# A decoder block on one core: the last output block's chain in column halves, its roots on ScalarE and VectorE, and two weight sums in the output stage

## The chip, the core and the metric

The kernel runs on one core of a Trainium2 chip. The metric is device time in microseconds: the median of three runs of the kernel before is 1132.89 us (1131.26 to 1133.38). One more execution was profiled. It took 1129.9 us, its span on the engines is 1128.1 us, and every time in the text that is read from an instruction is in us from that span's start. TensorE is called PE in the profile, VectorE DVE, ScalarE ACT, GpSimd POOL, and SyncE, which issues the DMAs, SP.

## What is computed

One transformer block over 1024 tokens of width 1024, in fp32. `rms_norm` divides by the root of the mean square and multiplies by a gain.

```python
h = rms_norm(x, g_attn_pre[l]) * (1 + sc_a) + sh_a
proj = h @ w_in[l]
...
mixed = jnp.concatenate([rms_norm(oa, g_mix_a[l]), rms_norm(ob, g_mix_b[l])], axis=-1)
y = mixed @ w_out[l]
x = x + gt_a * rms_norm(y, g_attn_post[l])

h = rms_norm(x, g_mlp_pre[l]) * (1 + sc_m) + sh_m
y = jnp.square(jax.nn.relu(h @ w_up[l])) @ w_down[l]
x = x + gt_m * rms_norm(y, g_mlp_post[l])
```

`oa` and `ob` are the results of two attention mixers with 512 columns each; the hidden width of the MLP is 4096.

## The kernel before

The kernel has three stages. Input projection and attention take the first 395 us. The output stage (`w_out`, both norms, the residual) follows to about 498 us. The MLP fills the rest.

**Products in parts.** A matrix product is made of three TensorE passes. Each operand is split into a high part, a cast by ScalarE, and a low part, the difference by VectorE, which needs the cast. The passes are high by high, high by low and low by high. In the MLP `split` (L1855 on) makes the parts: the cast is L1868 and the low part L1875, or L1866 and L1872 where an operand comes in two pieces of columns.

**The output stage.** `out_block` runs for eight blocks of 128 tokens, numbered 0 to 7. It loads the mixers' result (`o_sb`, L1625) and the residual (`x_sb`, L1629), makes the parts `oh` (ScalarE, L1638) and `ol` (VectorE, L1641), and squares and sums the mixers' result for their norms: a square on ScalarE (L1643), two additions on VectorE (L1647, L1648), a tiny product `pm_o` on TensorE (L1654), and a root, which is a first step on VectorE (`rs_t`, L1662) and a power of -0.5 on GpSimd (L1664). The product with `w_out` (`y_ps`, L1680 to L1682) is 16 groups of three matmuls; ScalarE (L1695) and VectorE (L1701) bring its halves of 512 columns to `y_sb`.

Then comes the block's chain. ScalarE squares `y` and sums (L1708); VectorE makes `rs_t` (L1717); GpSimd takes the power (L1719); VectorE multiplies by root and gate (L1723) and adds the residual (L1726), which SP stores (L1728); ScalarE squares again (L1708), `rs_t` and power follow again (L1717, L1719), and ScalarE scales by the root (`xn`, L1734). TensorE transposes `xn` (`px`, L1743, eight transposes), and ScalarE (L1759) and VectorE (L1762) scale, shift and store the result in quarters of the MLP's left operand: "11" and "12" are tokens 0 to 511 with either half of the features, "21" and "22" are tokens 512 to 1023. Each quarter lies in two tiles, 0 and 1.

**The MLP.** It multiplies in seven products per half of a pass instead of eight, in the order P1, P2, P6, P5, P7, P3, P4. P1 takes left quarter "11" with weight quarter "11", P2 takes "12" with "21"; both need only tokens 0 to 511. P6 takes S2 with T2. S1 = "21" + "22" and S2 = S1 - "11" are sums of left quarters, which need all tokens (`first_sums`, L1994, L1999, L2017); T1 = "12" - "11" and T2 = "22" - T1 are sums of weight quarters (`add_up`, L2037). In the first half T1 is written over weight quarter "11", whose parts must be made first, and the additions are queued when P6 is set up. The matmuls are L2104 to L2106, the results are read by L2138 to L2144.

**What sets the order.** A list scheduler in the kernel (`Sched`) fixes, when the program is built, the order of instructions of each engine. It knows a modelled duration of each step, its dependences, its tokens for memory, and a number `prio`; on each engine `pick` takes the step that can start earliest, with a handicap by `prio`. On the chip each engine runs its list in that order, so an instruction that waits holds up all behind it on its engine, and DMAs on SP's list too. On TensorE the last block's `px` stands behind 45 matmuls after block 6's `px` (all but one group of three of them from P1), and the other 45 matmuls of P2 behind it.

The first weight quarters are loaded in the order `RAW` (L2216), each behind the store of one block: the first behind block 2's, the last behind block 5's (L1849).

Of the kernel before, what the change touches and what calls it, by code (L numbers as in the profile page):

```python
# [10 lines left out]
F32 = mybir.dt.float32  # L11
# [171 lines left out]
class Step:  # L183
    __slots__ = ("dur", "emit", "deps", "takes", "gives", "prio", "seq", "ev", "alts", "after", "kind", "gone", "n", "lag")


class Sched:
# [11 lines left out]
    def step(self, dur, emit, deps=(), takes=(), gives=(), prio=5, after=None, kind="", n=1, lag=0.0):  # L199
        o = Step()  # L200
        o.n, o.lag = n, lag
        o.dur, o.emit, o.deps, o.takes, o.gives = dur, emit, deps, takes, gives
        o.prio, o.after, o.kind, o.ev, o.gone = prio, after, kind, Ev(), False
        o.seq = self.seq
        self.seq += 1
        return o
# [37 lines left out]
    def give_out(self, e, o, start):  # L244
# [12 lines left out]
        o.ev.t = end + o.lag  # L257
# [8 lines left out]
    def pick(self, e):  # L266
        best = None
        q = self.queue[e]
# [92 lines left out]
def hybrid_block(ctx: ExitStack, tc: tile.TileContext, x, positions, w_ada, b_ada, g_attn_post, w_in, w_out,  # L361
# [1226 lines left out]
    def open_h2():  # L1588
# [4 lines left out]
        ph2.right = pool("ring_r", 24, "right")  # L1593
        r_stg.give(sc.clk["PE"], NSTG2)
        r_raw.give(sc.clk["PE"], 10)
# [21 lines left out]

    def out_block(tb):
        b = {}

        late = tb >= TB - 2

# [88 lines left out]
        def norm(col, dep):  # L1711
            bx = []

            def f1():
# [6 lines left out]
        e = op("ACT", t_sb(D) + AP_COST, f_sq(0, True), ey, prio=1)  # L1721
        e = norm(0, e)
        e = op("DVE", t_dv(D), lambda: V.scalar_tensor_tensor(b["y"][:], b["y"][:], b["st"][:, 1:2], ph2.gate[:],  # L1723
                                                              ALU.mult, ALU.mult), [e, ph2.e_gate],
               gives=[(r_u, 1)] if tb == TB - 1 else [], prio=1)
        e = op("DVE", t_dv(D), lambda: V.tensor_tensor(b["y"][:], b["y"][:], b["xt"][:], ALU.add), [e, ex],  # L1726
               gives=[(r_stg, 1)], prio=1)
        e_x2[tb] = load(lambda: nc.sync.dma_start(x2_dram[tb][:], b["y"][:]), 524288, [e], prio=-2)  # L1728
        e = op("ACT", t_sb(D) + AP_COST, f_sq(2, False), [e], prio=1)
        e = norm(2, e)  # L1730

        def f_xn():
            b["xn"] = ring_l("xn2", F32)
            A.mul(b["xn"][:], b["y"][:], b["st"][:, 3:4])  # L1734
        exn = op("ACT", t_sb(D) + AP_COST, f_xn, [e], takes=[(ph2.r_xn, 1)], prio=1)
        ph2.pending_y = getattr(ph2, "pending_y", []) + [(exn, e_x2[tb], r_u if late else ph2.r_y)]
        et = []
        for kg in range(2):
# [5 lines left out]
            et.append(pe_op("xt", 0.43, f_t, [exn], takes=[(r_t, 1)],  # L1744
# [28 lines left out]
    def free_y():  # L1773
        for p_ in list(getattr(ph2, "pending_y", [])):
            if p_[0].t is not None and p_[1].t is not None:
                p_[2].give(max(p_[0].t, p_[1].t))
                ph2.pending_y.remove(p_)
# [56 lines left out]
    def load_raw(h, q):  # L1834
# [5 lines left out]
        for j in range(2):  # L1840
# [8 lines left out]
            deps = [halves[h - 1].e_b["T2"][j]] if h else [e_x2[2 + RAW.index(q)]]  # L1849
# [5 lines left out]
    def split(prio, rec, side, src, deps, free, pieces=None):  # L1855
# [3 lines left out]
        for i, c in enumerate(pieces or (slice(0, 512),)):  # L1859
            for j in range(2):  # L1860
# [21 lines left out]
                e1 = op("ACT", t_as(n), hi, d + (evs[j] or []), takes=[] if i else [(r_hl, 1)], prio=prio)  # L1882
                evs[j] = [e1, op("DVE", t_dv(n), lo, [e1], prio=prio,
# [24 lines left out]
    def sums(h, p):  # L1908
# [5 lines left out]
        if p == "P1":  # L1914
            fr.update({"T1": joins(r_raw, 2), "T3": joins(r_raw, 1), "B22": joins(r_raw, 3), "T4": joins(r_raw, 1),
                       "T2": joins(r_raw, 2)})
# [17 lines left out]
        if p == "P6":  # L1934
            sum_(t.b, t.e_b, eb, r_raw, None, "T1", "12", "11", ALU.subtract, [], t.sp["B", "11"], "11")
            sum_(t.b, t.e_b, eb, r_raw, ring_r, "T2", "22", "T1", ALU.subtract, [fr["B22"], fr["T1"]], None, None)
# [15 lines left out]
    def prep(h, p, rec):  # L1952
# [8 lines left out]
        fb = [fr["B22"]] if b == "22" else [fr[b]] if b in last_b else []  # L1961
# [65 lines left out]
    def add_up(prio, tiles, evs, ev, ring, new, out, x, y, alu, free, before, place):  # L2027
# [254 lines left out]
```

## Time and profile before

| what | us |
|---|---|
| median of the runs shown | 1132.89 (1131.26 to 1133.38) |
| the profiled execution | 1129.9 |
| its span | 1128.1 |
| TensorE busy | 1093.0 |
| VectorE, ScalarE, GpSimd busy | 813.5, 633.3, 264.9 |
| TensorE busy from 497.7 to 530 | 27.27 of 32.3 |
| TensorE busy from 530 to 1128 | 588.21 of 598 |

A row of the timeline gives start and duration in us, the engine, the line, the operation, what it writes and reads (tile names without their numbers), the shape, and how many like it were drawn together (x8); in brackets stands how long the engine was idle before, and whose result ended it. A row of the groups gives total busy us and the mean in ns. A row of the windows gives, for a stretch of time, the busy us of each engine with the number of instructions, then the TensorE clock granted as a share of full speed, the DMA share and GB/s.

### The profile page before, as it was taken

The page shows a single profiled execution, that of the slowest core. Times are in us where ns is not written, and L with a number is a line of the kernel's source. Part 1 is how long each engine was busy: PE and PEld are TensorE (multiplying, and loading weights), DVE is VectorE, ACT ScalarE, POOL GpSimd, SP SyncE. Part 2 cuts the span into 40 slices and gives each one's busy share as a digit, 9 for nine tenths or more (in the row PEclk, how much of TensorE's full clock was granted, in tenths as well). Part 3 has the DMA queues.
Part 4 walks back from the last instruction along what each step waited for, and adds up shares of the span by engine and source line. Part 5 has one row for each costly group of instructions (what it writes and reads, how often), then busy time and mean ns, then how long its engine had stood idle before and what let it go on. Part 6 is the DMA issues. An engine that isn't in the chain of part 4 may idle for free.

```text
span 1128.1 us, 15345 instructions
## 1 busy us (share of the span) xinstructions
PE 1093.0 (97%) x5280; PEld 905.8 (80%) x5280; DVE 813.5 (72%) x1427; ACT 633.3 (56%) x1146; POOL 264.9 (23%) x360
## 2 busy tenths in 40 slices
PE   9999999999999699998999999999999999999996
PEld 7777888888888578876888888888888888888885
DVE  7868776767667755688789554798643996537998
ACT  7959866655546756676575335653145632247542
POOL 2347767685744511111000000000000000000001
PEclk9999999999999799999999999999999999999998
DMA  9675655453634244653961269611578113584104
GB/s 337 190 227 155 182 176 189 155 180 124 196 129 141 90 131 154 211 203 146 341 242 38 75 234 324 235 56 38 191 263 301 38 57 111 188 315 150 38 19 150
DMA packets 93597, 189.54 MB, mean 168 GB/s; under 512 B 8528, under 2 KB 33232, under 8 KB 93520
## 3 DMA queue, kind: packets, MB, share of 16 engines
q1 hardware_dynamic: 93520, 188.57, 48.3%
q8 instruction: 42, 0.69, 0.3%
q14 instruction: 35, 0.29, 0.1%
HBM read 139.25 MB, written 30.41 MB: 150 GB/s over the span
## 4 chain that ended last, share of the span: by engine, by line
PE 75%; DVE 10%; ACT 5%; POOL 4%; issue 3%; DMA 2%; SPq 0%; DVEq 0%; POOLq 0%; ACTq 0%
PE mlp_ps L2105 17%; PE mlp_ps L2106 17%; PE mlp_ps L2104 17%; PE pj L889 4%; PE pj L892 3%; PE pj L890 3%; PE s_ps L1208 1%; PE acc L906 1%; DVE hw L1875 1%; DMA o_sb<-o_dram 1%; POOL ada_acc L1042 1%; PE o_ps L1492 1%; PE o_ps L1393 1%; PE s_ps L1301 1%; PE acc L892 1%
## 5 line engine op out<-in xcount | busy, mean ns | idle before, releaser
L2104 PE MATMUL mlp_ps<-hw 128*128 128x512 f32 x896 | 350.3, 391 | 0.4 <-ACT hw L1866 0.4
L2105 PE MATMUL mlp_ps<-hw 128*128 128x512 f32 x896 | 349.1, 390 | 1.1 <-DVE hw L1872 1.1
L2106 PE MATMUL mlp_ps<-hw 128*128 128x512 f32 x896 | 349.0, 390 | 0.0
L2105 PEld LDWEIGHTS mlp_ps<-hw 128*128 128x128 f32 x896 | 168.5, 188 | 36.8 <-DVE hw L1872 1.4
L2104 PEld LDWEIGHTS mlp_ps<-hw 128*128 128x128 f32 x896 | 168.6, 188 | 36.2 <-ACT hw L1866 0.8
L2106 PEld LDWEIGHTS mlp_ps<-hw 128*128 128x128 f32 x896 | 168.5, 188 | 35.1
L1875 DVE TENSOR_TENSOR hw<-w,hw 128x1024 fp32r<-128x1024 f32 x96 | 114.7, 1222 | 94.6 <-ACT hw L1868 94.3
L1868 ACT CAST hw<-w 128x1024 fp32r<-128x1024 f32 x96 | 97.5, 1047 | 129.8 <-PE mlp_ps L2106 93.1
L2204 POOL TENSOR_TENSOR st<-st,nhalf 128x1 f32<-128x1 f32 x8 | 7.8, 978 | 602.8 <-DVE st L2202 602.8
L889 PE MATMUL pj<-hw,w_hl 128*128 128x512 f32 x240 | 102.7, 428 | 2.0 <-ACT vt L839 2.0
L892 PE MATMUL pj<-hw,w_hl 128*128 128x512 f32 x240 | 95.0, 396 | 0.0
L890 PE MATMUL pj<-hw,w_hl 128*128 128x512 f32 x240 | 94.7, 395 | 0.0
L1868 ACT CAST hw<-u 128x1024 fp32r<-128x1024 f32 x48 | 48.7, 1051 | 64.6 <-PE mlp_ps L2106 64.6
L1875 DVE TENSOR_TENSOR hw<-u,hw 128x1024 fp32r<-128x1024 f32 x48 | 57.1, 1221 | 18.2 <-ACT hw L1868 18.2
L2162 DVE TENSOR_TENSOR yacc<-yacc,mlp_ps 128x512 f32<-128x512 f32 x96 | 62.2, 684 | 3.3 <-PE mlp_ps L2106 3.3
L1042 POOL TENSOR_TENSOR ada_acc<-ada_acc,wa_st 128x512 f32<-128x512 f32 x42 | 56.1, 1336 | 3.5
L892 PEld LDWEIGHTS pj<-hw,w_hl 128*128 128x128 f32 x240 | 45.3, 189 | 10.3
L1680 PE MATMUL y_ps<-hw,oh 128*128 128x512 f32 x128 | 51.2, 400 | 0.0
L889 PEld LDWEIGHTS pj<-hw,w_hl 128*128 128x128 f32 x240 | 45.7, 190 | 6.2 <-ACT vt L839 2.2
L1682 PE MATMUL y_ps<-hw,ol 128*128 128x512 f32 x128 | 50.0, 391 | 0.4 <-DVE ol L1641 0.4
L1681 PE MATMUL y_ps<-hw,oh 128*128 128x512 f32 x128 | 50.1, 391 | 0.0
L890 PEld LDWEIGHTS pj<-hw,w_hl 128*128 128x128 f32 x240 | 45.7, 190 | 3.8 <-issue 0.2
(238 smaller groups left out, 1960.7 us busy)
## 6 DMA issues: line engine op xcount, KB each, us to landing
hw<-s_dram SPq DMA_DIRECT2D x84, 512.0 KB, 4.2
wa_st<-in_w_ada SPq DMA_DIRECT2D x32, 512.0 KB, 4.3
w<-in_w_up SPq DMA_DIRECT2D x32, 512.0 KB, 4.9
w<-in_w_down SPq DMA_DIRECT2D x32, 512.0 KB, 7.3
s_dram<-hw SPq DMA_DIRECT2D x28, 512.0 KB, 3.8
qt<-hl SPq DMA_DIRECT2D x40, 256.0 KB, 2.5
w_st<-in_w_in SPq DMA_DIRECT2D x36, 256.0 KB, 3.1
x_sb<-in_x SPq DMA_DIRECT2D x16, 512.0 KB, 6.0
```

Source lines behind the costliest of these rows:

```text
L889: T.matmul(ps, w[:, 0, n], h[0], start=(k == 0), stop=False)
L890: T.matmul(ps, w[:, 1, n], h[0], start=False, stop=False)
L892: T.matmul(ps, w[:, 0, n], h[1], start=False, stop=(k == KC - 1))
L1042: G.tensor_tensor(ada.acc[:, :512], ada.acc[:, :512], wa[:, j], ALU.add)
L1680: T.matmul(ps[:], b["oh"][:, k], wh[:, c0:c0 + 512], start=(k == 4 * m), stop=False)
L1681: T.matmul(ps[:], b["oh"][:, k], wl[:, c0:c0 + 512], start=False, stop=False)
L1868: A.copy(out[j][0], flat(src[j]))
L1875: V.tensor_tensor(out[j][1], flat(src[j]), out[j][0].bitcast(F32), ALU.subtract)
L2104: T.matmul(ps[m][:], sh, mh, start=starts and k == 0, stop=False, **kw)
L2105: T.matmul(ps[m][:], sh, ml_, start=False, stop=False, **kw)
L2106: T.matmul(ps[m][:], sl, mh, start=False, stop=k == 3, **kw)
L2162: e = op("DVE", t_dv(512), lambda: V.tensor_tensor(y(), y(), ps[m][:], ALU.add), [e, ml.e_y[tb, n]], gives=gives, prio=1)
```

## The change

For the last block (7) a new function, `last_chain`, takes the place of the chain. It works on two halves of 512 columns. ScalarE squares each half as it is evicted; VectorE multiplies each half by the gate before the root is known; the root is made without GpSimd, by three small VectorE steps on the sums, ScalarE's square root, VectorE's reciprocal and two more small steps that refine it. One VectorE instruction for each half then makes root times product plus residual. The second root goes the same way. ScalarE makes the first half of `xn`, VectorE the second, and each group of four transposes waits for its own half. Square root needs a table on ScalarE; a dummy square root loads it in the time of block 2's chain.

The four additions of the first half's T1 and T2 (128x1024 each) leave P6 and are queued as soon as the weight quarters are there. T1 gets tiles of its own (two more in `ring_r`). The quarters are loaded two blocks earlier and in the order "11", "12", "22", "21". `pick` may now pass over its choice for a step with a higher `crit` that can start before half of the choice's duration is over: 3 for the last chain, 0 for all else, -1 for the early additions. In `split`, where an operand comes in two pieces, the cast of the second piece no longer waits for the low part of the first.

```diff
     def pick(self, e):
+        best = self.first(e, self.queue[e])
+        while best:
+            o = best[2]
+            over = [c for c in self.queue[e] if c.crit > o.crit]
+            urgent = self.first(e, over) if over else None
+            if not urgent or urgent[1] >= best[1] + 0.5 * (o.alts[e][0] if o.alts else o.dur):
+                break
+            best = urgent
+        return best
...
-        ph2.right = pool("ring_r", 24, "right")
+        ph2.right = pool("ring_r", 26, "right")
         r_stg.give(sc.clk["PE"], NSTG2)
-        r_raw.give(sc.clk["PE"], 10)
+        r_raw.give(sc.clk["PE"], 12)
...
+    def last_chain(b, ey, ex):
+        hs = (slice(0, 512), slice(512, 1024))
+        kw = dict(prio=-1, crit=3)
+
+        def sq(i, col, dep):
+            def f():
+                if not col and not i:
+                    b["st"] = small.tile([P, 8], F32, name="st_l", tag="st_l")
+                A.activation(ph2.junk[:, hs[i]], b["y"][:, hs[i]], AF.Square, accum_out=b["st"][:, col + i:col + i + 1])
+            return op("ACT", t_as(512) + 0.19, f, dep, **kw)
+
+        def norm(col, e0, e1):
+
+            def c(i):
+                return b["st"][:, col + i:col + i + 1]
+            e0 = op("DVE", 0.1, lambda: V.tensor_scalar(c(0), c(0), 1.0 / D, EPS, ALU.mult, ALU.add), [e0], **kw)
+            e1 = op("DVE", 0.2, lambda: V.scalar_tensor_tensor(c(2), c(1), 1.0 / D, c(0), ALU.mult, ALU.add), [e0, e1],
+                    **kw)
+            eh = op("DVE", 0.1, lambda: V.tensor_scalar(c(1), c(2), -0.5, None, ALU.mult), [e1], **kw)
+            e1 = op("ACT", 0.22, lambda: A.activation(c(2), c(2), AF.Sqrt), [e1, eh], **kw)
+
+            def f1():
+                V.reciprocal(c(2), c(2))
+                V.scalar_tensor_tensor(c(1), c(1), c(2), c(2), ALU.mult, ALU.mult)
+                V.scalar_tensor_tensor(c(2), c(1), 1.5, c(2), ALU.add, ALU.mult)
+            return op("DVE", 0.65, f1, [e1], **kw)
+        s0 = sq(0, 0, [ey[0]])
+        s1 = sq(1, 0, [ey[1], s0])
+        eg = []
+        for i in range(2):
+            def f_g(i=i):
+                if not i:
+                    b["xn"] = ring_l("xn2", F32)
+                V.tensor_tensor(b["xn"][:, hs[i]], b["y"][:, hs[i]], ph2.gate[:, hs[i]], ALU.mult)
+            eg.append(op("DVE", t_dv(512), f_g, [ey[i], ph2.e_gate] + eg, takes=[] if i else [(ph2.r_xn, 1)],
+                         gives=[(r_u, 1)] if i else [], **kw))
+        er = norm(0, s0, s1)
+        es, ew = [], []
+        for i in range(2):
+            def f_x(i=i):
+                V.scalar_tensor_tensor(b["y"][:, hs[i]], b["xn"][:, hs[i]], b["st"][:, 2:3], b["xt"][:, hs[i]],
+                                       ALU.mult, ALU.add)
+            ew.append(op("DVE", t_dv(512) + AP_DV, f_x, [er, eg[i], ex, s0, s1], gives=[(r_stg, 1)] if i else [], **kw))
+            es.append(sq(i, 4, [ew[i]] + es))
+        e_x2[TB - 1] = load(lambda: nc.sync.dma_start(x2_dram[TB - 1][:], b["y"][:]), 524288, ew, prio=-2)
+        er = norm(4, *es)
+        return [op("ACT", t_as(512) + AP_COST, lambda: A.mul(b["xn"][:, hs[0]], b["y"][:, hs[0]], b["st"][:, 6:7]), [er],
+                   **kw),
+                op("DVE", t_d2(512) + AP_DV, lambda: V.tensor_scalar(b["xn"][:, hs[1]], b["y"][:, hs[1]], b["st"][:, 6:7],
+                                                                     1.0, ALU.mult, ALU.mult), [er], **kw)]
...
+        if tb == 4:
+            def f_set():
+                A.activation(small.tile([P, 8], F32, name="rs_t", tag="rs_t")[:, 0:1], ones[:, 0:1], AF.Sqrt)
+            op("ACT", 1.5, f_set, [e_x2[1]], prio=3)
...
+            exn = last_chain(b, ey, ex)
...
-            et.append(pe_op("xt", 0.43, f_t, [exn], takes=[(r_t, 1)],
+            et.append(pe_op("xt", 0.43, f_t, [exn[kg]], takes=[(r_t, 1)],
...
-            deps = [halves[h - 1].e_b["T2"][j]] if h else [e_x2[2 + RAW.index(q)]]
+            deps = [halves[h - 1].e_b["T2"][j]] if h else [e_x2[RAW.index(q)]]
...
-                e1 = op("ACT", t_as(n), hi, d + (evs[j] or []), takes=[] if i else [(r_hl, 1)], prio=prio)
-                evs[j] = [e1, op("DVE", t_dv(n), lo, [e1], prio=prio,
+                was = evs[j] or [None, None]
+                e1 = op("ACT", t_as(n), hi, d + was[:1] * bool(i), takes=[] if i else [(r_hl, 1)], prio=prio)
+                evs[j] = [e1, op("DVE", t_dv(n), lo, [e1] + was[1:] * bool(i), prio=prio,
...
         if p == "P6":
-            sum_(t.b, t.e_b, eb, r_raw, None, "T1", "12", "11", ALU.subtract, [], t.sp["B", "11"], "11")
-            sum_(t.b, t.e_b, eb, r_raw, ring_r, "T2", "22", "T1", ALU.subtract, [fr["B22"], fr["T1"]], None, None)
+            if h:
+                sum_(t.b, t.e_b, eb, r_raw, None, "T1", "12", "11", ALU.subtract, [], t.sp["B", "11"], "11")
+                sum_(t.b, t.e_b, eb, r_raw, ring_r, "T2", "22", "T1", ALU.subtract, [fr["B22"], fr["T1"]], None, None)
             if h == 0:
                 first_sums(t)
...
-    RAW = ("11", "21", "12", "22")
+    RAW = ("11", "12", "22", "21")
 
     def open_raw():
-        if not hasattr(ph2, "right") or len(e_x2) < 6:
+        if not hasattr(ph2, "right") or len(e_x2) < 4:
             return False
         for q in RAW:
             load_raw(0, q)
+        t = half(0)
+        t.free.update({"11": joins(r_raw, 2), "T1": joins(r_raw, 2), "B22": joins(r_raw, 3)})
+        sum_ = partial(add_up, 9, crit=-1)
+        eb = events(0)[1]
+        sum_(t.b, t.e_b, eb, r_raw, ring_r, "T1", "12", "11", ALU.subtract, [t.free["11"]], None, None)
+        sum_(t.b, t.e_b, eb, r_raw, ring_r, "T2", "22", "T1", ALU.subtract, [t.free["B22"], t.free["T1"]], None, None)
         return True
```

VectorE's order from the last block's first `rs_t` on, before. `hw` are parts, `w_0` and `w_1` weight tiles, `h_12_0` a left quarter's tile, `st` and `rs_t` the small tiles of the root.

```order
L1717 TENSOR_SCALAR rs_t<-st_5771 128x1
L1875 TENSOR_TENSOR hw<-w_1_5418,hw 128x1024
L1723 SCALAR_TENSOR_TENSOR y_sb<-y_sb,st_5771,gate_a 128x1024
L1875 TENSOR_TENSOR hw<-h_12_0_5102,hw 128x1024
L1726 TENSOR_TENSOR y_sb<-y_sb,x_sb_5589 128x1024
L1875 TENSOR_TENSOR hw<-h_12_1_5103,hw 128x1024
L2037 TENSOR_TENSOR w_1_5363<-w_1_5529,w_1_5363 128x1024
L1717 TENSOR_SCALAR rs_t<-st_5771 128x1
L2037 TENSOR_TENSOR sum_T_5844<-w_0_5631,w_0_5361 128x1024
L2037 TENSOR_TENSOR sum_T_5856<-w_1_5644,w_1_5363 128x1024
L1994 TENSOR_TENSOR sum_S_5864<-h_21_0_5537,h_22_0_5546 128x2x384
L1762 TENSOR_SCALAR h_21_0_5537<-px_5866,g_m,s_m 128x128 x2
```

The same place now. `st_l` is the small tile of the last chain, and `xn_5797` first holds y times gate.

```order
L1661 TENSOR_TENSOR xn_5797<-y_sb,gate_a 128x512
L1644 SCALAR_TENSOR_TENSOR st_l<-st_l 128x1
L1661 TENSOR_TENSOR xn_5797<-y_sb,gate_a 128x512
L1646 TENSOR_SCALAR st_l<-st_l 128x1
L1830 TENSOR_SCALAR h_22_0_5560<-px_5784,g_m,s_m 128x128 x2
L1830 TENSOR_SCALAR h_22_1_5561<-px_5784,g_m,s_m 128x128 x2
L1650 RECIPROCAL st_l<-st_l 128x1
L1651 SCALAR_TENSOR_TENSOR st_l<-st_l 128x1
L1652 SCALAR_TENSOR_TENSOR st_l<-st_l 128x1
L1668 SCALAR_TENSOR_TENSOR y_sb<-xn_5797,st_l,x_sb_5603 128x512 x2
L1643 TENSOR_SCALAR st_l<-st_l 128x1
L1943 TENSOR_TENSOR hw<-h_12_0_5102,hw 128x1024
```

Before, one low part stood behind the first `rs_t`, T1's second piece ahead of the second `rs_t`, and T2's two pieces (`sum_T`) and S1's first behind it. Now there is no step of GpSimd between the rows, only low parts and block 6's evictions, and the T additions are gone from here; the second root follows behind the low parts of the left quarter "12".

VectorE's order from block 3's residual addition on, before: one low part stands ahead of the eviction of the next block, and sums of the next block's `o_sb` behind `rs_t`.

```order
L1726 TENSOR_TENSOR y_sb<-y_sb,x_sb_5145 128x1024
L1641 TENSOR_TENSOR ol<-o_sb,oh 128x1024
L1701 SCALAR_TENSOR_TENSOR y_sb<-y_ps,rab,y_sb 128x512
L1717 TENSOR_SCALAR rs_t<-st_5336 128x1
L1647 TENSOR_TENSOR o_sb<-o_sb 128x2x256
L1648 TENSOR_TENSOR o_sb<-o_sb 128x2x128
```

The same place now; `px_5422` is block 3's.

```order
L1792 TENSOR_TENSOR y_sb<-y_sb,x_sb_5145 128x1024
L1766 SCALAR_TENSOR_TENSOR y_sb<-y_ps,rab,y_sb 128x512
L1782 TENSOR_SCALAR rs_t<-st_5354 128x1
L2108 TENSOR_TENSOR sum_T_5401<-w_0_5324,sum_T_5237 128x1024
L1706 TENSOR_TENSOR ol<-o_sb,oh 128x1024
L2108 TENSOR_TENSOR sum_T_5418<-w_1_5337,sum_T_5249 128x1024
L1830 TENSOR_SCALAR h_11_0_5093<-px_5422,g_m,s_m 128x128 x2
```

The second `rs_t` of block 3 has T2's two additions behind it and the low part `ol` of block 5 between them, which stood ahead of `rs_t` before. In the same way T1's two additions stand on both sides of block 2's first `rs_t`.

TensorE's order around block 3's transposes, before; `pm_o` belongs to block 5.

```order
L1682 MATMUL y_ps<-hw,ol 128x512
L1654 MATMUL pm_o<-ones,o_sb 128x1 x2
L1743 MATMUL px_5411<-head,xn_5398 128x128 x4
L1743 MATMUL px_5421<-head,xn_5398 128x128 x4
L1680 MATMUL y_ps<-hw,oh 128x512
```

The same place now.

```order
L1747 MATMUL y_ps<-hw,ol 128x512
L1811 MATMUL px_5422<-head,xn_5407 128x128 x4
L1811 MATMUL px_5428<-head,xn_5407 128x128 x4
L1745 MATMUL y_ps<-hw,oh 128x512
L1746 MATMUL y_ps<-hw,oh 128x512
```

The tiny product `pm_o` of block 5 has moved from ahead of block 3's transposes to behind twelve matmuls that follow them; block 2's transposes stand nine matmuls later than they did.

## The prediction on record

> **What bounds the kernel now.** I read the busy times first, then what TensorE waits for in the stretch that the change touches, then that stretch instruction by instruction on each engine, last the granted clock there.
>
> ```profile
> span 1128.1 us, 15345 instructions
> PE 1093.0 (97%) x5280; PEld 905.8 (80%) x5280; DVE 813.5 (72%) x1427; ACT 633.3 (56%) x1146; POOL 264.9 (23%) x360
> ```
>
> TensorE is busy for 97% of the span, so a gain can only come out of the 35 us in which it isn't, or out of time at a lower clock. The waits of TensorE from 470 to 532 us (us in total, times, longest), the seam between output stage and MLP:
>
> ```profile
> PE px L1743 <- ACT xn L1734: 3.5, 2, 3.0
> PE mlp_ps L2105 <- DVE hw L1872: 1.1, 1, 1.1
> PE mlp_ps L2104 <- ACT hw L1866: 0.4, 1, 0.4
> ```
>
> The same on TensorE's timeline (start, duration, in brackets the idle time before); px at 499.52 belongs to block 6, px at 513.90 to the last block, and the last rows are the end of P2 and the start of P6:
>
> ```profile
> 499.52 1.09 PE L1743 MATMUL px<-head,xn 128*128 128x128 f32 x8 [0.51 <-ACT xn L1734]
> ...
> 510.47 0.39 PE L2106 MATMUL mlp_ps<-hw 128*128 128x512 f32 x1
> 513.90 1.55 PE L1743 MATMUL px<-head,xn 128*128 128x128 f32 x8 [3.04 <-ACT xn L1734]
> ...
> 526.45 0.39 PE L2106 MATMUL mlp_ps<-hw 128*128 128x512 f32 x1
> 527.20 0.50 PE L2104 MATMUL mlp_ps<-hw 128*128 128x512 f32 x1 [0.37 <-ACT hw L1866]
> 528.82 0.50 PE L2105 MATMUL mlp_ps<-hw 128*128 128x512 f32 x1 [1.12 <-DVE hw L1872]
> 529.16 0.39 PE L2106 MATMUL mlp_ps<-hw 128*128 128x512 f32 x1
> ```
>
> The granted clock (the number before the last two) in single microseconds of it:
>
> ```profile
> 513.00:514.00 1.00, 0.10 (x1) 0.11 (x2) 0.00 (x0) 1.00 (x2) 0.00 (x0) 1.00 0.00 0
> 515.00:516.00 1.00, 1.00 (x5) 0.91 (x4) 1.00 (x5) 1.00 (x2) 0.00 (x0) 0.50 0.00 0
> 518.00:519.00 1.00, 1.00 (x6) 0.79 (x5) 0.38 (x2) 0.83 (x1) 0.00 (x0) 1.00 0.00 0
> ```
>
> **What goes.** Three pieces. (1) The last block's px waits 3.04 us. (2) After that wait the clock is 0.50, and back at 1.00 by 518. Px of block 6 with the 45 matmuls behind it takes from 499.52 to the end of the slot of 510.47 (0.23 us, the spacing of these matmuls): 11.18 us. The last block's px with the 45 of P2 behind it takes from 513.90 to 526.68: 12.78. The clock cost 1.60. (3) P6's third matmul would start at 526.45 + 3 x 0.227 = 527.13 and starts at 529.16: 2.03. Sum 6.67 us.
>
> The Trainium skill, page "TensorE: Matmul & The Clock Gate", Part 1, has the clock at half after an idle window of about 3.4 us that runs freely. By it a 3.04 us wait need not be caught in every execution, and the sum would lose 1.60 where it isn't. The trace shows it caught once, so I keep the 1.60, and the range covers its absence.
>
> Why is xn late? DVE, POOL and ACT around the last root, and two POOL roots elsewhere to compare:
>
> ```profile
> 508.98 0.15 DVE L1717 TENSOR_SCALAR rs_t<-st 128x1 f32<-128x1 f32 x1
> 509.04 2.35 DVE L2037 TENSOR_TENSOR sum_T<-w,w 128x1024 f32<-128x1024 f32 x2
> 511.31 0.95 DVE L1994 TENSOR_TENSOR sum_S<-h,h 128x768 f32<-128x768 f32 x1
> ```
>
> ```profile
> 456.42 0.55 POOL L1719 TENSOR_TENSOR st<-rs_t,nhalf 128x1 f32<-128x1 f32 x1 [4.51 <-DVE rs_t L1717]
> 496.82 1.46 POOL L1719 TENSOR_TENSOR st<-rs_t,nhalf 128x1 f32<-128x1 f32 x1 [7.14 <-DVE rs_t L1717]
> 509.20 3.46 POOL L1719 TENSOR_TENSOR st<-rs_t,nhalf 128x1 f32<-128x1 f32 x1 [6.00 <-DVE rs_t L1717]
> ```
>
> ```profile
> 496.66 1.22 DVE L2037 TENSOR_TENSOR w<-w,w 128x1024 f32<-128x1024 f32 x1
> ```
>
> A power of 128 numbers takes 0.55 us on POOL with DVE quiet, but ends 0.40 us after the DVE addition that runs beside it (497.88 and 498.28), or after a whole run of three (512.26 and 512.66). The additions of sum_T and sum_S stand right behind the root's first step and so hold the root up by 2.9 us.
>
> **The last block's chain now.** It has no POOL step. I run it by hand along the order of DVE and ACT, from the last eviction of y and with these durations:
>
> ```profile
> 497.79 1.41 DVE L1701 SCALAR_TENSOR_TENSOR y_sb<-y_ps,rab,y_sb 128x512 f32<-128x512 f32 x2
> ```
>
> ```profile
> L2179 ACT ACTIVATE junk<-yacc 128x512 bf16<-128x512 f32 x16 | 10.1, 630 | 20.9 <-DVE yacc L2162 20.7
> L1169 DVE RECIPROCAL den<-den 128x1 f32<-128x1 f32 x32 | 5.0, 159 | 8.4 <-ACT p_sb L1166 8.2
> L1262 ACT ACTIVATE d_far<-d_far 128x16 f32<-128x16 f32 x8 | 1.7, 214 | 6.7 <-DVE d_far L1259 6.7
> L632 DVE TENSOR_SCALAR x_sb<-x_sb,rstd 128x1024 f32<-128x1024 f32 x4 | 3.0, 752 | 2.4 <-POOL rstd L473 2.4
> ```
>
> ACT is free of block 6's xn at about 499.4; two half squares at 0.63, with the read of the sum behind each, end at 500.1 and 500.9. DVE, in its order, has a weight's low part (1.22, to 501.4), two products y*gate and the small steps (to 502.7), four evictions of block 6 (1.37, to 504.1). ACT's square root (0.21) lies beside these; reciprocal and two small steps (0.15 each) end at 504.5, both halves of y (1.41) at 505.9. ACT squares each half as it comes, to 506.7. DVE fills with one low part of h (to 507.3) and, the sum's small steps between, another (to 508.6); reciprocal and two steps to 509.1. Xn half 1 on DVE, about half of 0.75, is there at 509.5; half 0 on ACT waits for the cast of a T2 piece that stands ahead of it and is there at 510.35. TensorE is free at 510.47 + 0.23 + 0.16 = 510.86 (the rows' own 513.90 less 3.04). So piece (1) goes whole, with 0.5 us to spare, and piece (2) with it.
>
> Piece (3): px then starts at 510.86 and P2 ends 11.18 later, at 522.0. P6 needs the S2 sums, which wait for px, and T2's parts, whose additions are no longer there. DVE gets through its rows up to the first low part of S2 by 521.5 in the same hand run, and to the second, needed at about 527, by 525.6. The first has only 0.5 us of cover; each half microsecond of a late eviction beyond that is paid. I put 0.2 for it, between 0 and the 2.03 of before. The order dropped between high and low parts costs nothing: the casts run earlier in ACT's idle time, and the P6 rows are where it would pay.
>
> **What comes: the four T additions in the output stage.** Each is 1.22 on DVE. Rows around blocks 2 and 3 of before:
>
> ```profile
> 438.79 0.54 POOL L1719 TENSOR_TENSOR st<-rs_t,nhalf 128x1 f32<-128x1 f32 x1 [4.36 <-DVE rs_t L1717]
> ```
>
> ```profile
> 436.59 0.75 DVE L1701 SCALAR_TENSOR_TENSOR y_sb<-y_ps,rab,y_sb 128x512 f32<-128x512 f32 x1 [1.23 <-PE y_ps L1682]
> ...
> 456.19 0.14 DVE L1717 TENSOR_SCALAR rs_t<-st 128x1 f32<-128x1 f32 x1
> ```
>
> ```profile
> 457.00 1.15 ACT L1734 ACTIVATE xn<-y_sb,st 128x1024 f32<-128x1024 f32 x1 [0.28 <-POOL st L1719]
> ```
>
> ```profile
> 457.51 0.39 PE L1682 MATMUL y_ps<-hw,ol 128*128 128x512 f32 x1
> 458.04 0.58 PE L1654 MATMUL pm_o<-ones,o_sb 128*128 128x1 f32 x4
> 458.48 1.07 PE L1743 MATMUL px<-head,xn 128*128 128x128 f32 x8
> ```
>
> T1's first piece fits into the DVE gap behind the eviction of 436.59. Its second stands behind block 2's first root: DVE 438.7 to 439.9, POOL to 440.3 instead of 439.33. The chain is 0.9 us later; block 2's px stands 9 matmuls later now (2.0 us) and covers it, pm_o of block 4 does not quite: 0.24 us.
>
> T2's first piece stands right behind block 3's second root: DVE 456.29 to 457.51, POOL to 457.9 instead of 456.97. Xn then runs 457.95 to 459.1. Px was 0.3 us behind its xn before (xn's end 458.15, px 458.48), so it starts at 459.14, 0.66 later; and 0.44 of pm_o (458.04 to 458.48), which used to lie ahead of px, is still to do. Together 1.10 us, the 0.24 included. This supposes that POOL gets in at the boundary to the next DVE instruction, the low part `ol`. One place shows a root getting in between such instructions, at the kernel's end:
>
> ```profile
> 1097.76 2.13 POOL L2204 TENSOR_TENSOR st<-st,nhalf 128x1 f32<-128x1 f32 x2 [585.10 <-DVE st L2202]
> ```
>
> ```profile
> 1097.67 0.69 DVE L2199 TENSOR_TENSOR yg<-yacc,gate_m 128x512 f32<-128x512 f32 x1
> 1098.27 2.35 DVE L1875 TENSOR_TENSOR hw<-u,hw 128x1024 fp32r<-128x1024 f32 x2
> ```
>
> Two roots were done by 1099.89 while DVE ran on to 1100.62. Like there, the follower of T2's first piece is a low part; so I take this, and not the run of three at 509.04.
>
> The Trainium skill, page "SBUF — State Buffer", section "SBUF: two separate sides", has a port pair that DVE with two SBUF inputs or GpSimd holds for a whole instruction, the other blocked. The rows of 496.66 and 496.82 agree for one addition; the 3.46 us at 509.20 are longer than one instruction. The rule speaks against this change, since it puts such additions behind two POOL roots; by it the sum is the one taken.
>
> The rest has one answer each. The table load and dummy root (1.28 and 0.2 us, estimated from the load at the kernel's start, 1283 ns) stand where ACT is idle between a cast and a square. The weight loads, two blocks earlier on SP's queue, are cheap if they land before T1's first piece (a rival below). In the MLP the sum and its loads stand as before, and TensorE waits nowhere behind 530.
>
> ```profile
> L585 ACT ACT_TABLE_LOAD x1 | 1.3, 1283 | 0.7 <-PEq L2272 0.7
> ```
>
> **Sum.** -6.67 + 1.10 + 0.2 = -5.4 us (rounded). The profiled execution took 1129.9, so 1124.5; the median shown is 1132.89, so 1127.5.
>
> **Rivals.** A: as summed, 1127.5, chance 0.50. B: POOL isn't held at block 3 at all, because its root's step of 128 numbers comes through first; then only the 0.24 is paid: -6.67 + 0.24 + 0.2 = -6.2, 1126.7, chance 0.17. The row of 496.82 speaks against it. C: the root is held through the whole DVE run there, T2, `ol`, T2, to 459.79 + 0.40 = 460.2, as at 509.20. Xn ends at 461.4, px starts 461.45: 2.97 later, with 0.44 of pm_o 3.41, and an idle time of 3.3 us, so the half clock again, 1.60: -6.67 + 5.01 + 0.2 = -1.5, 1131.4, no difference that can be told. Chance 0.16: two rows of this trace, one each way. D: px or P6 at the seam keeps part of its wait, since the hand run has eight hand-overs between ACT and DVE: each late by 0.2 is 1.6, of which 0.5 is covered; -5.4 + 1.1 to +2 gives 1128.6 to 1129.5, chance 0.12. E, slower: T1's first piece waits for the weight quarter "12", and DVE being in order, block 2's root and all behind it wait too.
>
> ```profile
> 429.34 0.32 SPq L1728 DMA_DIRECT2D x_dram<-y_sb  x1
> ```
>
> ```profile
> w<-in_w_up SPq DMA_DIRECT2D x8, 512.0 KB, 5.6
> ```
>
> The quarter's loads go out behind block 1's store, about 429.7 and 430.4, and land 5.6 us later, at 436; DVE wants them at 437.3. Every microsecond of a landing beyond 437.3 is paid once; the change is slower than before only from 437.3 + 5.4 = 442.7 on, by 0.2% from 445. A landing at 447, eleven microseconds late, would give 1137. Chance 0.05.
>
> A measurement of this kernel tells about 0.2%, 2.3 us, from no change. Faster by more are A, B and D: 0.50 + 0.17 + 0.12 = 0.79, and the part of C in which the half clock isn't caught, 0.03: 0.82. Within 0.2%: the rest of C, 0.13. Slower: 0.05. The range reaches from B less the spread of the runs shown (1.2) to C: 1125.5 to 1131.8.
>
> **What would show it.** Right: px of the last block with no wait, no clock below 1.00 around it, P6 without the waits on L1866 and L1872 of before, a wait of about 1 us at block 3's px with the POOL root there 1.4 long. Wrong: POOL's root behind block 3 over 3 us long (C) or 0.55 (B); a px wait left at the seam (D); DVE idle on a DMA ahead of block 2's root (E).

## The result, and the profile after

The changed kernel took 1123.49 us (median of four runs, 1122.45 to 1124.64); the kernel before, with a fourth run, 1133.14 (1131.26 to 1134.46). The ratio is 0.9922, with a 95% interval of 0.9904 to 0.9940. That is faster, as forecast, but the time is 2.0 us below the forecast's range of 1125.5 to 1131.8. Between the two profiled executions there are 5.75 us, 1129.9 against 1124.15, where 5.4 was forecast.

What TensorE waits for from 470 to 532 us, after (us in total, times, longest):

```profile
PE px L1811 <- ACT xn L1800: 0.5, 1, 0.5
PE pm_o L1719 <- DVE o_sb L1713: 0.2, 1, 0.2
```

The one px wait left is block 6's. On TensorE's timeline after: px of block 6, the last px, the last matmul of P2 (522.78) and the third of P6 (523.46).

```profile
500.74 1.09 PE L1811 MATMUL px<-head,xn 128*128 128x128 f32 x8 [0.50 <-ACT xn L1800]
...
511.69 0.39 PE L2177 MATMUL mlp_ps<-hw 128*128 128x512 f32 x1
511.92 1.03 PE L1811 MATMUL px<-head,xn 128*128 128x128 f32 x8
...
522.78 0.39 PE L2177 MATMUL mlp_ps<-hw 128*128 128x512 f32 x1
523.01 0.39 PE L2175 MATMUL mlp_ps<-hw 128*128 128x512 f32 x1
523.23 0.39 PE L2176 MATMUL mlp_ps<-hw 128*128 128x512 f32 x1
523.46 0.39 PE L2177 MATMUL mlp_ps<-hw 128*128 128x512 f32 x1
```

No wait stands ahead of the last px, and P6 follows P2 at the spacing of 0.23 us. The windows after the last px have the full clock:

```profile
513.00:514.00 1.00, 1.00 (x6) 0.81 (x5) 1.00 (x4) 1.00 (x5) 0.00 (x0) 1.00 1.11 317
514.00:515.00 1.00, 1.00 (x6) 0.84 (x5) 1.00 (x3) 1.00 (x3) 0.00 (x0) 1.00 0.90 342
```

The price at block 3, after, on three engines: the second root's first step with T2's addition behind it, the power on GpSimd, and px.

```profile
456.61 0.15 DVE L1782 TENSOR_SCALAR rs_t<-st 128x1 f32<-128x1 f32 x1 [0.46 <-ACT junk L1773]
456.68 1.22 DVE L2108 TENSOR_TENSOR sum_T<-w,sum_T 128x1024 f32<-128x1024 f32 x1
457.81 1.22 DVE L1706 TENSOR_TENSOR ol<-o_sb,oh 128x1024 fp32r<-128x1024 f32 x1
```

```profile
456.84 1.46 POOL L1784 TENSOR_TENSOR st<-rs_t,nhalf 128x1 f32<-128x1 f32 x1 [4.08 <-DVE rs_t L1782]
```

```profile
459.53 1.09 PE L1811 MATMUL px<-head,xn 128*128 128x128 f32 x8 [0.84 <-ACT xn L1800]
```

The root ends at 458.30, 0.40 behind T2's addition (457.90) and inside `ol`. Px waits 0.84, where the prediction's case A had about 1 us. T1's first piece runs right behind the eviction ahead of it, without a wait for its weights, so the prediction's case E isn't there:

```profile
437.70 1.22 DVE L2108 TENSOR_TENSOR sum_T<-w,w 128x1024 f32<-128x1024 f32 x1
```

**A ruler for the experiments.** Block 0's px starts at 420.74 before and 421.21 after:

```profile
420.74 1.07 PE L1743 MATMUL px<-head,xn 128*128 128x128 f32 x8
```

```profile
421.21 1.07 PE L1811 MATMUL px<-head,xn 128*128 128x128 f32 x8
```

All that the change moves lies behind it: up to it the compute engines have the same instructions in the same order, and the first of the moved weight loads goes out at 421.97. From there to the end of the span before takes 1128.1 - 420.74 = 707.36 us, after 1122.3 - 421.21 = 701.09: -6.27. Second profiles of the same two kernels gave 707.42 and 701.15. So this stretch, which the text calls the ruler, repeats within 0.06 us in kernels whose times spread over ten, and shows what the runs can't. Each of the other kernels was profiled once. The parts of the stretch, in us (px0 is block 0's px, px7 the last; "P6" is P6's third matmul; the first column is from the span's start):

| kernel | to px0 | px0 to px6 | px6 to px7 | px7 to P6 | P6 to end | px0 to end |
|---|---|---|---|---|---|---|
| before | 420.74 | 78.78 | 14.38 | 15.26 | 598.94 | 707.36 |
| after | 421.21 | 79.53 | 11.18 | 11.54 | 598.84 | 701.09 |
| before again | 421.08 | 78.80 | 14.38 | 15.25 | 598.99 | 707.42 |
| after again | 424.25 | 79.52 | 11.17 | 11.55 | 598.91 | 701.15 |
| warm wait | 427.43 | 78.78 | 14.38 | 14.41 | 600.50 | 708.07 |
| last chain, parts' order | 418.62 | 78.74 | 11.17 | 16.60 | 600.37 | 706.88 |
| sums, parts' order | 423.00 | 79.57 | 14.72 | 14.46 | 598.95 | 707.70 |
| parts' order alone | 427.37 | 78.75 | 14.39 | 15.27 | 598.92 | 707.33 |
| after, parts' old order | 423.69 | 79.53 | 11.17 | 13.77 | 598.94 | 703.41 |
| after, GpSimd roots | 419.20 | 79.47 | 9.03 | 15.03 | 598.87 | 702.40 |
| after, T2 in halves | 425.51 | 79.11 | 11.18 | 11.54 | 598.86 | 700.69 |
| after, T in the gaps | 424.83 | 78.39 | 11.18 | 11.54 | 598.86 | 699.97 |

### The profile page after: what moved, and what is told of

It is laid out like the page before. It is cut to its first block, busy times and chain, and to the rows that moved or that the text cites. A ratio compares the mean times of both kernels' runs of the same rounds, so it can differ in the third digit from the quotient of the medians.

```text
span 1122.3 us, 15352 instructions
## 1 busy us (share of the span) xinstructions
PE 1089.2 (97%) x5280; PEld 903.9 (81%) x5280; DVE 816.3 (73%) x1436; ACT 636.0 (57%) x1158; POOL 260.2 (23%) x358
## 4 chain that ended last, share of the span: by engine, by line
PE 75%; DVE 8%; ACT 5%; POOL 4%; DMA 3%; issue 3%; SPq 1%; DVEq 0%; POOLq 0%; ACTq 0%
PE mlp_ps L2175 17%; PE mlp_ps L2176 17%; PE mlp_ps L2177 17%; PE pj L899 3%; PE pj L902 3%; PE pj L900 3%; PE s_ps L1218 1%; DMA wa_st<-in_w_ada 1%; POOL ada_acc L1052 1%; PE o_ps L1502 1%; DMA o_sb<-o_dram 1%; PE acc L902 1%; PE acc L899 1%; PE pt_ps L1467 1%; PE acc L900 1%
## 5 line engine op out<-in xcount | busy, mean ns | idle before, releaser
L1943 DVE TENSOR_TENSOR hw<-w,hw 128x1024 fp32r<-128x1024 f32 x94 | 112.4, 1222 | 95.5 <-ACT hw L1936 95.2
```

Of the source, the lines that this page charges most:

```text
L1943: V.tensor_tensor(out[j][1], flat(src[j]), out[j][0].bitcast(F32), ALU.subtract)
```

## The experiments

The theory at the start: the change does what the prediction says, and the rest of the gain is the clock in other stages, which differs from run to run. The rival: the change gains at a place that the prediction doesn't name. The table speaks for the first theory: of the 6.27 us all but 0.1 lie between px0 and P6, and what lies between the medians beyond that, 9.65 us in all, isn't in this stretch in either pair of profiles.

### The two kernels again

No edit; twelve more runs of before and six of after, one of each profiled.

> The kernel before, unchanged, with a second profile. Theory C (clock): the profiled execution of before (1129.9 us) lost less to the half clock at the seam than the timed ones (1131.3 to 1134.5). Then this profile, if it is slower than 1129.9, has the difference in the stretch 510 to 530 us or in other stretches with a clock under 1.00, and its mean granted clock is under 0.988. Rival S (spread): the difference lies evenly over the stages (each stage longer by 0.1 to 0.4%) at the same clock. Ratio to before by both: 1.000 within 0.002.

> The changed kernel once more, with a second profile. Theory W (windows): the half clock comes in pieces of 3.41 us, each costing 1.71 us; the change takes away one or two of them at the seam, 3.2 us of px wait and 2.0 of P6 wait, adds 0.75 at blocks 2 and 3, and the remaining spread of the times is the number of such pieces in the attention stage, which differs from run to run. Then the stretch from block 0's px to the last px is 90.7 us again within 0.1 (before 93.2), no clock under 1.00 lies between 395 us and the kernel's end, and the median is 1123.5 to 1126 against 1131 to 1132 of before: ratio 0.993 to 0.996. Rival L (luck): the four runs were low by chance, the median is above 1126, and the ratio above 0.996.

Before again: 1131.77 us (1129.48 to 1135.20), ratio 1.0001 (0.9986 to 1.0016). After again: 1126.52 (1122.10 to 1127.31), ratio 0.9948 (0.9930 to 0.9965). The stretch and the clock are as theory W has them (90.7 us from px0 to px7, full clock from 395 us to the last matmul), but luck had a part too: the median is above 1126, though the ratio isn't above 0.996. The two profiles of before are too close to decide between the theories of the first expectation: they are 0.4 us apart, 0.34 of it ahead of px0, with the same clock of 0.988 and the same seam. With every run of this study, before has a median of 1131.7 (63 runs, standard deviation 2.2) and after 1124.8 (10 runs, 2.0). Their difference of 6.9 holds the 6.27 of the ruler well within what ten runs can tell.

Where does the spread come from? The windows of the changed kernel's profile and of the slowest profile (warm wait, 1137.34 us), over stretches of the attention stage (the third is put around the half clock that ends the stage in each); the clock is the number before the last two:

```profile
111.00:116.00 5.00, 5.00 (x33) 4.15 (x32) 5.00 (x13) 2.60 (x6) 5.00 (x9) 1.00 0.74 239
316.00:324.00 8.00, 8.00 (x45) 6.92 (x45) 6.38 (x25) 4.88 (x16) 3.33 (x2) 1.00 0.09 27
377.00:391.00 14.00, 9.30 (x36) 7.11 (x34) 10.98 (x35) 9.39 (x24) 9.04 (x10) 0.51 0.25 75
```

```profile
111.00:116.00 5.00, 5.00 (x21) 3.59 (x22) 3.88 (x8) 2.20 (x5) 4.60 (x4) 0.66 0.69 207
316.00:324.00 8.00, 7.84 (x29) 6.98 (x30) 2.15 (x9) 2.10 (x7) 2.05 (x2) 0.57 0.04 8
381.00:399.00 18.00, 12.21 (x41) 9.17 (x41) 13.69 (x43) 11.87 (x34) 9.94 (x11) 0.53 0.21 62
```

The clock that a window loses is its length times one minus the clock; it costs as much time only where TensorE is busy throughout, which it isn't in the third window (9.30 of 14 us, 12.21 of 18). After loses 14 x 0.49 = 6.9 us here; warm wait loses 5 x 0.34 = 1.7, 8 x 0.43 = 3.4 and 18 x 0.47 = 8.5. All are multiples of 1.7: the half clock comes in pieces of 3.4 us. The twelve profiles have four to eight such pieces ahead of px0, and px0 starts between 418.6 us (four pieces) and 427.4 (eight). The number of pieces isn't all of it: after has four as well, and px0 at 421.2. That stage the change doesn't touch. The first four runs of after had granted clocks of 0.988 to 0.991, those of before lie between 0.982 and 0.989, and over 59 runs of before that have their clock listed, the time falls by 1.2 us for each 0.001 of it (correlation -0.82).

### The wait kept warm

```diff
                 b["px", kg] = pt.tile([P, 4, P], F32, name="px2", tag="t")
+                if tb == TB - 1 and not kg:
+                    for k in range(12):
+                        T.matmul(b["px", kg][:, k % 4], ident, ident, start=True, stop=True)
```

> The kernel before with 12 products of 128x128 by 128x128 (0.22 us each, 2.6 in all, into the tile that the transposes then overwrite) put on TensorE ahead of the last block's px: the wait for xn is still there, but TensorE is busy in it. Nothing else moves. Both theories: no half clock behind px. Theory C: the time falls by all that the clock loses there in ordinary executions, 1.6 us by the first profile and up to 1.6 + 3.9 = 5.5 us. Rival S: by 1.6 us, and the 3.9 us by which the change gained more than its profile shows are found elsewhere. If the half clock does nothing: 0.

Neither theory held: 1132.91 us, ratio 1.0010 (0.9994 to 1.0027). The third forecast, 0, has the right number, but not for its reason. The clock behind px is 1.00, and still the time didn't fall. The profile's waits behind the last px up to 540 us, and its clock behind P6's start:

```profile
PE mlp_ps L2107 <- ACT hw L1869: 1.2, 1, 1.2
PE mlp_ps L2108 <- DVE hw L1875: 1.1, 1, 1.1
```

```profile
535.00:538.50 3.50, 3.50 (x10) 2.72 (x9) 3.50 (x5) 2.21 (x3) 0.00 (x0) 0.52 0.92 358
```

P2 ended 1.6 us earlier behind px, but P6's third matmul came only 0.85 earlier (14.41 against 15.26): P6's two waits together grew from 1.5 to 2.3 us. Now a piece of half clock follows them (P6 to end 600.50, 1.6 longer), and by the ruler the kernel is 0.7 slower. About half of what the clock gives back is lost in the waits behind it, and the rest in the new piece: here it is worth nothing as long as those waits stay. The prediction could add the two because the change takes away both.

### One part at a time

The last chain with the parts' order (the four T additions back at P6, weight loads as before). The dropped order between the parts stays dropped here, the new `pick` stays too, as in all kernels below that are made from the changed one, and two tiles of `ring_r` are unused:

```diff
-            if h:
+            if True:
                 sum_(t.b, t.e_b, eb, r_raw, None, "T1", "12", "11", ALU.subtract, [], t.sp["B", "11"], "11")
...
-        sum_(t.b, t.e_b, eb, r_raw, ring_r, "T1", "12", "11", ALU.subtract, [t.free["11"]], None, None)
-        sum_(t.b, t.e_b, eb, r_raw, ring_r, "T2", "22", "T1", ALU.subtract, [t.free["B22"], t.free["T1"]], None, None)
...
-    RAW = ("11", "12", "22", "21")
+    RAW = ("11", "21", "12", "22")
```

> The last block's chain in halves alone: the four T additions back at P6, weight quarters loaded in the order and at the time of before. By the prediction's sum the px wait (3.04) and the half clock (1.60) go, P6's 2.03 stays in part, since VectorE has two T2 additions and the S sums in the way again, and nothing is added at blocks 2 and 3: -4.6 to -6.7 us by the profiles. Theory C: up to 3.9 us more against timed runs of before, -8.5 to -10.6. Rival: without the T additions moved, VectorE's backlog makes px or P6 wait 2 us or more, and the gain is under 4 us.

The rival's forecast, a gain under 4 us, came out: 1132.28 us, ratio 0.9996 (0.9976 to 1.0016), by the ruler 0.5 us less than before. The last px waits for nothing, but P6 does:

```profile
PE mlp_ps L2175 <- DVE hw L1940: 3.4, 1, 3.4
PE mlp_ps L2174 <- ACT hw L1934: 1.0, 1, 1.0
```

VectorE, which hardly idles from 503.24 on, has the additions, the sums of S and evictions ahead of S2's low parts, which start here:

```profile
522.48 2.49 DVE L1940 TENSOR_TENSOR hw<-sum_S,hw 128x768 fp32r<-128x768 f32 x4
```

So the wait moves 16 us on, with its own piece of half clock.

The T additions and the parts' order, with the chain of before:

```diff
...
-        if tb < TB - 1:
+        if True:
...
```

> The T additions in the output stage and the dropped order of the parts, with the last block's chain as before (whole columns, power on GpSimd). VectorE has a sum of S and two low parts (0.95 + 1.22 + 1.22) behind the last root's first step, so by the row of 509.20 the root is held again for about 3 us and px waits 2 to 3 us, with the half clock; P6's 2.03 goes at least in part; 1.1 is added at blocks 2 and 3. Together -1 us (between -3 and +1). Rival: a low part lets the root in after 1.5 us, as at the kernel's end, px waits about 1 us without half clock: -4 us.

The first forecast came out: 1132.56 us, ratio 1.0004 (0.9989 to 1.0019), by the ruler 0.3 us more than before. VectorE's rows behind the last root's first step, and the root itself:

```profile
512.37 0.15 DVE L1782 TENSOR_SCALAR rs_t<-st 128x1 f32<-128x1 f32 x1
512.43 0.95 DVE L2070 TENSOR_TENSOR sum_S<-sum_S,h 128x768 f32<-128x768 f32 x1
513.30 2.36 DVE L1943 TENSOR_TENSOR hw<-sum_T,hw 128x1024 fp32r<-128x1024 f32 x2
```

```profile
512.60 3.46 POOL L1784 TENSOR_TENSOR st<-rs_t,nhalf 128x1 f32<-128x1 f32 x1 [6.34 <-DVE rs_t L1782]
```

The root ends 0.40 behind this run of three (515.66 and 516.06), px waits 3.40 us, and P6 for nothing.

The parts' order alone, in before, and its reverse, the changed kernel with the old order:

```diff
...
-                e1 = op("ACT", t_as(n), hi, d + (evs[j] or []), takes=[] if i else [(r_hl, 1)], prio=prio)
+                e1 = op("ACT", t_as(n), hi, d + was[:1] * bool(i), takes=[] if i else [(r_hl, 1)], prio=prio)
...
```

> The kernel before with only the order between the parts of a split operand dropped. Theory B (backlog): P6 waits in before because VectorE still has T2's additions and the sums of S in front of the low parts; the dropped order alone changes little: from block 0's px to the end 707.4 us as in before, or down to 706.9. Rival O (order): the dropped order alone takes the 2 us that putting it back costs in the changed kernel: 705.4.

> The changed kernel with the order between parts put back: the cast of the second piece waits for the low part of the first. The prediction put this at nothing: P6 waits 0 to 0.2 us. Rival: with the casts later, P6's matmuls wait for a low part or a cast of S2, 0.5 us or more.

Alone it is worth nothing (ruler 707.33; one run, 1136.51 us with eight pieces ahead of px0). Put back in the changed kernel it costs 2.3 us (703.41; one run, 1128.88): P6 waits again.

```profile
PE mlp_ps L2175 <- DVE hw L1940: 2.0, 1, 2.0
```

### Which engine makes the last roots

```diff
...
-            e1 = op("ACT", 0.22, lambda: A.activation(c(2), c(2), AF.Sqrt), [e1, eh], **kw)
...
+            return op("POOL", 0.35, lambda: G.tensor_tensor(c(2), c(2), nhalf[:, :1], ALU.pow), [e1], **kw)
...
```

> The changed kernel with the last chain's halves kept, but its two roots by GpSimd's power, as in before (two small VectorE steps, then the power; no square root, no table). Behind the first root's step VectorE has one product of 512 columns, behind the second a low part of 1024. Theory G (the engine of the root matters): GpSimd is held as at the seam of before, 2 to 3.5 us at a root, and the last px waits 1.5 to 4 us again. Rival H (the place matters): each root is held by the one instruction behind it only, about 1.0 and 1.5 us, no longer than the ScalarE root with its three VectorE steps takes (1.9 us from 503.81 to 505.75), and px waits less than 0.3 us: from block 0's px to the end 701.1 us within 0.3, as in the changed kernel.

One run, 1123.42 us; the ruler has 702.40, 1.3 more than after. The two roots:

```profile
501.30 0.92 POOL L1646 TENSOR_TENSOR st_l<-st_l,nhalf 128x1 f32<-128x1 f32 x1 [3.87 <-DVE st_l L1644]
505.43 1.46 POOL L1646 TENSOR_TENSOR st_l<-st_l,nhalf 128x1 f32<-128x1 f32 x1 [3.21 <-DVE st_l L1644]
```

In the changed kernel the first root's last steps on VectorE, with block 6's evictions between them, and the last step to `xn` on ScalarE:

```profile
503.81 0.15 DVE L1646 TENSOR_SCALAR st_l<-st_l 128x1 f32<-128x1 f32 x1
503.87 1.36 DVE L1830 TENSOR_SCALAR h<-px,g_m,s_m 128x128 f32<-128x128 f32 x4
...
505.59 0.16 DVE L1652 SCALAR_TENSOR_TENSOR st_l<-st_l 128x1 f32<-128x1 f32 x1
```

```profile
510.83 0.72 ACT L1674 ACTIVATE xn<-y_sb,st_l 128x512 f32<-128x512 f32 x1
```

As H has it, each power is held by one instruction only; but VectorE's next instruction waits for the root itself, so a longer hold couldn't show here. `xn` is there 9.0 us behind px6, where the chain with ScalarE's roots takes 10.8 (500.74 to 511.55); the order of VectorE's other work differs too, so not all of the 1.8 us need be the roots. So the roots needn't leave GpSimd for this chain to be early. Px waits 1.10 all the same, because it stands 30 matmuls behind px6 in place of 45: the scheduler, which counts 0.35 for a power, had put it earlier. H's forecasts for that wait and for the end failed on that.

### Where the T additions stand

```diff
-        sum_(t.b, t.e_b, eb, r_raw, ring_r, "T1", "12", "11", ALU.subtract, [t.free["11"]], None, None)
+        sum_(t.b, t.e_b, eb, r_raw, ring_r, "T1", "12", "11", ALU.subtract, [t.free["11"]], [[e_y[2]], [e_y[3]]], None)
...
+               [[e_y[4]], [e_y[5]]], None, crit=-1)
```

> The changed kernel with the four T additions each behind one eviction of y, where VectorE waits 1.2 us for the sum of squares: pieces of T1 in blocks 2 and 3, of T2 in blocks 4 and 5. None stands behind a root's first step. If the 0.75 us at blocks 2 and 3 are the roots held up by these additions, the stretch from block 0's px to block 6's px falls from 79.5 to 78.8 us, as before, with all roots there 0.55 long, and the px wait of 0.84 is gone; the last px and P6 still wait for nothing. Timed: 0.7 us less than the changed kernel, less than the runs can tell. Rival: the shift comes from pm_o and px changing places on TensorE, and stays.

The first forecast held, and px0 to px6 is 0.4 lower still: no root of the chains of blocks 2 to 5 is longer than 0.55, px0 to px6 is 78.39, the ruler 699.97, 1.1 less than after. Timed 1124.52 us (1120.76 to 1126.87), ratio to before 0.9928 (0.9910 to 0.9945), beside 0.9948 of after in the same runs. It is the best version here by the ruler; by the times it can't be told from after.

```diff
...
+                    if crit and out == "T2":
+                        for c in (slice(0, 512), slice(512, 1024)):
+                            g.tensor_tensor(flat(tiles[out][j])[:, c], flat(tiles[x][j])[:, c], flat(tiles[y][j])[:, c], alu)
...
```

> The changed kernel with each of T2's two additions in the output stage done as two additions of 512 columns, one right behind the other. Theory R (run): a root that is held stays held to the end of a run of fp32 additions that wait for nothing: GpSimd's root at block 3 ends 0.4 us behind the second half, is about 1.5 us long, and px waits 0.8 to 1.0 us. Theory I (instruction): the root gets in at the first boundary: about 0.9 us long, and px waits 0.2 to 0.4.

Theory I held: px waits 0.32, and the root, ending 0.40 behind the first half, gets in between the two.

```profile
460.96 1.28 DVE L2110 TENSOR_TENSOR sum_T<-w,sum_T 128x512 f32<-128x512 f32 x2
```

```profile
461.12 0.92 POOL L1784 TENSOR_TENSOR st<-rs_t,nhalf 128x1 f32<-128x1 f32 x1 [4.09 <-DVE rs_t L1782]
```

One run, 1128.01 us.

## Why the prediction was right or wrong

- **The mechanism was right at each place it named.** Px7's wait, the half clock and P6's wait are gone; block 3's root is held by one instruction; case A it was. The table gives -3.20 from px6 to px7 (forecast -3.04), -3.72 from px7 to P6 (forecast -1.60 - 2.03 + 0.2 = -3.43), +0.75 from px0 to px6 (forecast +1.10), -0.1 behind. Taking the half clock into the sum rested on one trace; before has the wait and a piece behind it in each of its two profiles.
- **What failed is the sizing: first, of the sum, which was 0.9 too small.** It is -6.27 by the ruler against -5.4. Mis-sized were the 1.10 for blocks 2 and 3 (0.75: block 3's px comes 0.58 later behind px0 where 0.66 was forecast, and the 0.44 of `pm_o` behind it costs 0.17), the 0.2 kept for P6 (nothing), and 0.16 at px: without a wait it starts 0.23 behind the matmul ahead of it (511.69 and 511.92), not behind that matmul's end 0.39 later, from which the row's 3.04 counts.
- **Second, of the range, which failed at its lower end.** It was put at case B less 1.2 us, "the spread of the runs shown", three of them, of which the lowest lies 1.63 under the median; its upper end, 1131.8, is 0.4 above case C without a reason given. 63 runs of before spread from 1128.67 to 1139.77. A median of few runs carries one or two microseconds from the attention stage, in the forecast's anchor as in the result: 1132.89 is 1.2 over the median of 63, 1123.49 is 1.3 under that of ten. The anchor of 63 less the ruler's 6.27 is 1125.4. So of the 4.0 us between 1127.5 and 1123.49 the sum has 0.9, the anchor 1.2, and the low median of the four runs 1.9, which is the luck of few runs. Neither of the first two puts the result outside by itself: lowered by both, the range would begin at 1123.4.
- **"Profile against profile" agreed by luck in part.** The 5.75 us hold a piece at 313 us that before had and after had not, 1.7 us, and an attention stage that was otherwise slower in after (px0 0.47 later).
- **"The order dropped between high and low parts costs nothing" was an answer to the wrong question.** The prediction named P6 as the place where it would pay, but saw no gain in it; in the changed kernel it is worth 2.3 us, and 2.0 of P6's wait would have stayed without it (one profile).
- **The sum hid that its parts don't add.** The chain with the parts' order -0.5, the sums with the parts' order +0.3, the parts' order alone 0.0, all three -6.27. The chain and the sums weren't tried without the parts' order. The path through px7 and the one through T2 and S2 end at the same P6: with the chain shortened, P6 waits 1.03 and 3.37; with the sums moved, px7 waits 3.40. To shorten one shows the other.

What stays open: why a root is held through a whole run of VectorE instructions at the seam of before and of the sums' kernel (3.46 us, both times with VectorE busy without a gap ahead of the root's first step), and gets in after one at block 3, where VectorE runs on (at block 2 and in the GpSimd-roots kernel's last chain VectorE waits for the root itself, which shows neither). A gap ahead can't be all of it. At the kernel's end before has both cases within 6 us. VectorE has no gap there from 1092.17 on; each of the two roots that the prediction shows at 1097.76 got in after one instruction, but the next, at 1103.42, is held through two:

```profile
1103.42 1.59 POOL L2204 TENSOR_TENSOR st<-st,nhalf 128x1 f32<-128x1 f32 x1 [3.53 <-DVE st L2202]
```

```profile
1103.33 1.29 DVE L2199 TENSOR_TENSOR yg<-yacc,gate_m 128x512 f32<-128x512 f32 x2
```

It ends 0.39 behind them (1105.01 and 1104.62). The gap wasn't tried by itself. Nor was it settled what makes the number of half-clock pieces in the attention stage.

## What to carry to other kernels

When a wait is taken away, follow what ends second on each path to the next common point; here the chain and the sums were each worth next to nothing without the other. Measure such a change by a stretch of the trace between two fixed instructions around it, and take the range of a forecast for few runs from the spread of many. An addition that must be moved into a busy stage belongs where its engine waits for another, not behind the first step of a root.

## What the runs showed of the hardware

- The half clock comes in pieces of 3.4 us that cost 1.7 us each where TensorE is busy. At the seam one piece went with the wait of 3.04 us of before and, in the kernel of the chain with the parts' order, with 1.03 and 3.37; two with the wait of 3.40 in the sums' kernel; one with waits of 1.16 and 1.09 close together (warm wait). None followed 0.37 and 1.12 (before), 1.96 (the parts' old order) and 1.10 (GpSimd roots). The Trainium skill, page "TensorE: Matmul & The Clock Gate", Part 1, has a freely running window of about 3.4 us, which agrees with the size of a piece. What the prediction cites from it, that the clock is at half after an idle window, isn't borne out everywhere: once 1.16 and 1.09 were enough.
- GpSimd's power took 0.55 us with VectorE quiet. Beside a VectorE addition or product with two inputs from SBUF it ended 0.40 us behind it: 0.92 us long beside 512 columns, 1.46 beside 1024. In some places it ended 0.40 behind a run of two or three of them (1.59 and 3.46).
- A square root on ScalarE with reciprocal and two refining steps on VectorE took 1.9 us in this chain (503.81 to 505.75), but 1.36 of them are block 6's evictions on VectorE; from the reciprocal's start at 505.14 it is 0.6.
